# Gathered experts: u and v of an expert fetched as one 8 KB row instead of two 4 KB rows

## The chip, the cores and the metric

One core of a Trainium2 chip runs the kernel. The metric is device time in microseconds (us) of one execution; less is better. One execution was also taken by the hardware profiler, and all views below are of that one.

## What is computed

One layer of a diffusion backbone over 1024 latent tokens of width 1024: a token mixer (two recurrent scans), then PEER, a retrieval of experts. Only PEER is touched here. For each token, eight heads choose 16 experts each out of 16384, so 128 experts with an index and a gate. An expert is one row u and one row v of 1024 floats:

```
act = gelu(einsum('pd,ped->pe', hx, u_tab[ix]))        # one dot product per token and expert
y   = einsum('pe,ped->pd', gx * act, v_tab[ix])        # sum of 128 scaled rows v per token
x   = LN(ALPHA * x + g2 * y)
```

## The kernel before

The tokens form eight tiles of 128. PEER runs in two ways side by side.

**Dense tiles.** Tiles 0 to 4 (ND = 5, 640 tokens) are computed against all 16384 experts by TensorE, 128 steps of 128 experts. `dense_s` makes the products of h with u in a PSUM tile `S` (two halves of 24 matmuls) and ScalarE applies Gelu into `ge` (L1139). `dense_w` loads `vf`, splits it into two bf16 parts (ScalarE cast L1149, then a subtraction on POOL, L1150, that reads two SBUF tiles), multiplies `ge` by the gate matrix `G` (VectorE, L1152) and splits the product `w` (ScalarE L1154, VectorE L1155). `dense_y` sums four experts' w times v in a PSUM bank `y` (L1167), and VectorE adds it to `ya` in SBUF (L1174). `S` and `y` have three PSUM banks each. 66 of the 128 `S` steps are made ahead, while the gates are still being chosen, and spilled to DRAM.

**Gathered tiles.** Tiles 5 to 7 are computed by the class `Gather`, from rows fetched from DRAM by index: partition p receives the row that token p chose. `fetch` issues one indirect DMA on the POOL queue (L1075) for one of 256 steps of a tile: 128 rows u first, then 128 rows v, 4 KB for each partition, into a ring of six buffers `row` (ROWS). `use` takes the oldest. For a row u it is one VectorE instruction (L1094) that multiplies by h and sums into a column of `dot`; h lies in PSUM for this (copied once per tile, L1091). After 128 of them one Gelu on ScalarE (L1096) and one multiplication by the gates (L1097) serve the whole tile. For a row v it is one VectorE instruction (L1102) that adds the scaled row to a sum in the same two PSUM banks, `hg`. Their inputs in SBUF are thus one tile each, `row`; the other big operand is in PSUM.

`final` adds the residual, loads `xn` into a buffer of the same ring (L1110), normalizes and stores.

The order on each engine is set by a scheduler, from the program's order and its own estimate of times. `gather(n)` is called with a quota at each step of the other work: 100 rows while the scores are made (G0), 120 and 240 around the choice of gates (G1, G2), the rest of the 768 spread over the 128 dense steps. An engine works off its list in order: what waits at the head holds all behind it.

## Time and profile before

| what | value |
|---|---|
| median of 3 runs | 3173.94 us (3171.61 to 3189.06) |
| profiled execution, own time | 3190.5 us |
| its span, first to last instruction | 3188.7 us |
| busy: TensorE (PE), VectorE (DVE), POOL, ScalarE (ACT) | 91%, 79%, 58%, 37% |
| mean granted TensorE clock | 0.951 of 2.4 GHz |
| DMA: bytes, mean rate | 900.31 MB, 282 GB/s |

The gathered rows begin at about 1118 us, the matmuls of `dense_y` run from about 1900 to 3125 us, and the rest is the closing normalization. Busy shares are means over stages with different limits, so each stage is read by itself. PE busy counts the multiplying, with ends that are modelled; ACT, DVE, POOL busy count an instruction from its start to its end, with whatever held it up inside.

### The profile page before, as it was taken

The page shows a single profiled execution, that of the slowest core. Times are in us where ns is not written, and L with a number is a line of the kernel's source. Part 1 is how long each engine was busy: PE and PEld are TensorE (multiplying, and loading weights), DVE is VectorE, ACT ScalarE, POOL GpSimd, SP SyncE. Part 2 cuts the span into 40 slices and gives each one's busy share as a digit, 9 for nine tenths or more (in the row PEclk, how much of TensorE's full clock was granted, in tenths as well). Part 3 has the DMA queues.
Part 4 walks back from the last instruction along what each step waited for, and adds up shares of the span by engine and source line. Part 5 has one row for each costly group of instructions (what it writes and reads, how often), then busy time and mean ns, then how long its engine had stood idle before and what let it go on. Part 6 is the DMA issues. An engine that isn't in the chain of part 4 may idle for free.

```text
span 3188.7 us, 50415 instructions
## 1 busy us (share of the span) xinstructions
PE 2914.0 (91%) x18799; PEld 1889.2 (59%) x18943; DVE 2534.5 (79%) x5328; ACT 1194.3 (37%) x1743; POOL 1838.4 (58%) x1358
## 2 busy tenths in 40 slices
PE   7898999997698899999999989999999999999992
PEld 3644556666586567677777865554555555545550
DVE  8434464798778899898877778888888888888898
ACT  4464463445345522136666642221222122212211
POOL 3565675422347466416665665766666666666664
PEclk8999997998899899999999999999999999999996
DMA  7688666421268699859888998999999999989985
GB/s 282 211 291 291 214 211 218 166 79 42 100 228 278 219 332 345 295 188 309 295 289 296 309 358 314 361 337 340 357 366 365 360 362 361 360 329 372 357 319 190
DMA packets 319546, 900.31 MB, mean 282 GB/s; under 512 B 28076, under 2 KB 107572, under 8 KB 311364
## 3 DMA queue, kind: packets, MB, share of 16 engines
q1 hardware_dynamic: 208708, 494.38, 44.5%
q0 software_dynamic: 110592, 402.70, 33.9%
q8 instruction: 149, 2.44, 0.3%
q14 instruction: 97, 0.79, 0.1%
HBM read 758.67 MB, written 138.30 MB: 281 GB/s over the span
## 4 chain that ended last, share of the span: by engine, by line
PE 23%; DVE 22%; DMA 10%; issue 8%; POOL 6%; ACT 2%; SPq 1%; DVEq 0%; POOLq 0%; ACTq 0%
PE y L1167 12%; PE S L1134 9%; DMA row<-in_peer_v_dram,idx 7%; DVE row L1094 4%; POOL row L1075 3%; DVE hg L1102 3%; DMA row<-in_peer_u_dram,idx 2%; PE y L1042 2%; DVE us L1037 2%; POOL vs L1150 1%; DVE alt L881 1%; DVE ind L883 1%; DMA us<-in_peer_ut_dram 1%; DVE w L1155 1%; DVE ind L880 1%
## 5 line engine op out<-in xcount | busy, mean ns | idle before, releaser
L1134 PE MATMUL S<-hTd,uT 128*128 128x320 f16 (+1 forms) x6144 | 886.0, 301 | 0.5 <-ACT ge L1139 0.5
L1167 PE MATMUL y<-vs,w 128*128 128x512 bf16 x3730 | 852.2, 381 | 26.9 <-DVE ya L1174 11.0
L1134 PEld LDWEIGHTS <-uT 128*128 128x128 bf16 x6144 | 604.1, 98 | 251.9 <-issue 1.6
L1167 PEld LDWEIGHTS <-w 128*128 128x128 bf16 x3840 | 377.3, 98 | 460.7 <-issue 32.2
L1102 DVE SCALAR_TENSOR_TENSOR hg<-row,dot,hg 128x1024 f32<-128x1024 f32 x381 | 489.7, 1285 | 120.8 <-DMA row<-in_peer_v_dram,idx 117.1
L1075 POOL DMA_INDIRECT row<-in_peer_u_dram,idx x384 | 388.8, 1012 | 294.2 <-DVE row L1094 151.6
L1094 DVE SCALAR_TENSOR_TENSOR row<-row,hg 128x1024 f32<-128x1024 f32 x384 | 459.7, 1212 | 65.7 <-DMA row<-in_peer_u_dram,idx 63.4
L1075 POOL DMA_INDIRECT row<-in_peer_v_dram,idx x384 | 383.6, 999 | 219.3 <-DVE hg L1102 149.5
L199 POOL TENSOR_TENSOR uT<-us,uT 128x1024 bf16<-128x1024 f32 x128 | 297.4, 2328 | 186.4 <-ACT uT L198 170.9
L1149 ACT CAST vs<-vf 128x1024 bf16<-128x1024 f32 x128 | 130.3, 1043 | 510.5 <-PE y L1167 292.6
L1150 POOL TENSOR_TENSOR vs<-vf,vs 128x1024 bf16<-128x1024 f32 x128 | 276.4, 2176 | 41.0 <-ACT vs L1149 29.6
L1038 POOL TENSOR_TENSOR kT<-us,gf 128x512 f32<-128x512 bf16 x160 | 177.9, 1133 | 193.7 <-DVE us L1037 171.3
L1139 ACT ACTIVATE ge<-S 128x320 f32<-128x320 f32 x256 | 112.7, 442 | 402.2 <-PE S L1134 401.0
L222 PE MATMUL pj<-xmT,wb 128*128 128x512 f16 (+3 forms) x1214 | 251.4, 358 | 3.1 <-DVE q L500 0.9
L230 PE MATMUL pj<-wb,xmT 128*128 128x256 f16 (+1 forms) x1728 | 217.4, 286 | 15.1 <-DVE rsg L751 5.2
L1174 DVE TENSOR_TENSOR ya<-ya,y 128x512 f32<-128x512 f32 x310 | 208.8, 681 | 26.9 <-PE y L1167 26.3
L230 PEld LDWEIGHTS <-xmT 128*128 128x128 f16 (+1 forms) x1968 | 184.9, 103 | 54.8 <-issue 16.5
L1043 ACT COPY gst<-y 128x512 f32<-128x512 f32 x160 | 171.1, 1075 | 88.0 <-PE y L1042 88.0
L222 PEld LDWEIGHTS <-wb 128*128 128x128 f16 (+1 forms) x1248 | 121.2, 99 | 125.6 <-issue 21.2
L198 ACT CAST uT<-us 128x1024 bf16<-128x1024 f32 x128 | 133.3, 1044 | 135.2 <-DMA us<-in_peer_ut_dram 103.8
L1037 DVE TENSOR_TENSOR us<-iob,eT 128x512 bf16<-128x512 bf16 x320 | 166.7, 569 | 18.2 <-ACT kT L1039 9.2
L1042 PE MATMUL y<-kT 128*128 128x128 f32 x1280 | 163.1, 279 | 11.2 <-ACT kT L1039 6.5
(389 smaller groups left out, 3866.9 us busy)
## 6 DMA issues: line engine op xcount, KB each, us to landing
us<-in_peer_ut_dram SPq DMA_DIRECT2D x128, 512.0 KB
Ud<-uT SPq DMA_DIRECT2D x128, 512.0 KB
uT<-Ud SPq DMA_DIRECT2D x128, 512.0 KB
vf<-in_peer_v_dram SPq DMA_DIRECT2D x128, 512.0 KB
Gd<-gst SPq DMA_DIRECT2D x20, 1984.0 KB
Gt<-Gd SPq DMA_DIRECT2D x31, 1280.0 KB
Sd<-ge SPq DMA_DIRECT2D x66, 320.0 KB
kT<-Sd SPq DMA_DIRECT2D x66, 320.0 KB
```

The lines of the kernel that those rows point to most:

```text
L199: nc.gpsimd.tensor_tensor(lo, uf, hi, op=OP.subtract)
L222: g.nc.tensor.matmul(ps[:, :t1 - t0], w.t[a][:, k, c0:c0 + 128], g.xmT[b][:, k, t0:t1], start=(k == 0 and a == b), stop=(k == KD - 1 and a ...
L230: g.nc.tensor.matmul(ps, g.xmT[a][:, k, t * 128:(t + 1) * 128], w.t[b][:, k, :w.n], start=(k == 0 and a == b), stop=(k == KD - 1 and a == 1))
L1037: nc.vector.tensor_tensor(cm[:, a], g.iob, eT[:, a, None, t0:t0 + 4].to_broadcast([128, 128, 4]), op=OP.is_equal)
L1042: nc.tensor.matmul(ps[:, i * 128:(i + 1) * 128], oh[:, 0, i], oh[:, 1, i], start=True, stop=True)
L1075: d = g.nc.gpsimd.indirect_dma_start(out=b, out_offset=None, in_=self.I["peer_u" if n < 128 else "peer_v"][0], in_offset=bass.IndirectOffs ...
L1094: nc.vector.scalar_tensor_tensor(b, b, 1.0, self.ps, op0=OP.mult, op1=OP.mult, accum_out=dot[:, j:j + 1])
L1102: nc.vector.scalar_tensor_tensor(self.ps, b, dot[:, j:j + 1], self.ps, op0=OP.mult, op1=OP.add)
L1134: m = nc.tensor.matmul(ps[:, :hn], uT[:, a, k, :], g.hTd[b][:, k, i * hn:(i + 1) * hn], start=(k == 0 and (a, b) == (0, 0)), stop=(k == KD ...
L1150: nc.gpsimd.tensor_tensor(v[:, 1], vf, v[:, 0], op=OP.subtract)
L1167: nc.tensor.matmul(ps, w[:, a, t * 128:(t + 1) * 128], v[:, b, h * 512:(h + 1) * 512], start=(n == 0), stop=(n == 3 * GI - 1))
L1174: nc.vector.tensor_add(ya, ya, ps)
```

## The change

The host lays out a new input, `peer_uv`: row e is u of expert e followed by v of expert e, 2048 floats. One indirect DMA now brings both (128 steps of a tile, 384 in all), into a ring of four buffers of 8 KB for each partition; the quotas G0, G1, G2 are halved. The dot product reads h from SBUF (`g.h`), and PSUM holds only the sum (`sums`, two banks, made with the first row v). Gelu and the gate are applied to one column at a time on ScalarE, two instructions of 128x1 for each row (L1096, L1097). The addition of a row v stands in the program one step behind its dot product (`behind`). To make room, `ge` has two buffers instead of four, and `vf` one of its own and one of the pool `up`.

```
-        b = g.grp.tile([128, D], F32, name="row")
-        d = g.nc.gpsimd.indirect_dma_start(out=b, out_offset=None, in_=self.I["peer_u" if n < 128 else "peer_v"][0],
-                                           in_offset=bass.IndirectOffsetOnAxis(ap=g.idx[:, t, n % 128:n % 128 + 1], axis=0))
+        b = g.grp.tile([128, 2, D], F32, name="row")
+        d = g.nc.gpsimd.indirect_dma_start(out=b.rearrange("p a d -> p (a d)"), out_offset=None, in_=self.I["peer_uv"],
+                                           in_offset=bass.IndirectOffsetOnAxis(ap=g.idx[:, t, n:n + 1], axis=0))
...
-            nc.vector.scalar_tensor_tensor(b, b, 1.0, self.ps, op0=OP.mult, op1=OP.mult, accum_out=dot[:, j:j + 1])
-            if j == 127:
-                nc.scalar.activation(dot, dot, AF.Gelu)
-                nc.vector.tensor_mul(dot, dot, g.gate[:, t, :])
+            self.h = g.h[:, t, :]
+        dot = self.dot[:, j:j + 1]
+        nc.vector.scalar_tensor_tensor(b[:, 0], b[:, 0], 1.0, self.h, op0=OP.mult, op1=OP.mult, accum_out=dot)
+        nc.scalar.activation(dot, dot, AF.Gelu)
+        nc.scalar.activation(dot, dot, AF.Copy, scale=g.gate[:, t, j:j + 1])
+        if self.behind:
+            self.add()
+        self.behind = (t, j, b[:, 1], dot)
+    def add(self):
+        if j == 0:
+            self.ps = g.pb.tile([128, 2, 512], F32, name="sums").rearrange("p a b -> p (a b)")
+            nc.vector.tensor_scalar(self.ps, v, dot, None, op0=OP.mult)
         else:
-                nc.vector.scalar_tensor_tensor(self.ps, b, dot[:, j:j + 1], self.ps, op0=OP.mult, op1=OP.add)
+            nc.vector.scalar_tensor_tensor(self.ps, v, dot, self.ps, op0=OP.mult, op1=OP.add)
...
-    xt = g.grp.tile([128, D], F32, name="row")
+    xt = g.grp.tile([128, 2, D], F32, name="row")[:, 0]
...
-ROWS = 6
+ROWS = 4
...
-G0 = 100
-G1 = 120
-G2 = 240
+G0 = 50
+G1 = 60
+G2 = 120
...
-        g.gep = pool("gep", 4)
+        g.gep = pool("gep", 2)
...
-        g.vfp = pool("vfp", 2)
+        g.vfp = pool("vfp", 1)
...
+        g.vf = [g.vfp.tile([128, D], F32, name="vf"), g.up.tile([128, 2, D], BF, name="us").rearrange("p a b -> p (a b)").bitcast(F32)]
...
+    ins["peer_uv"] = np.stack([ins["peer_u"][0], ins["peer_v"][0]], axis=1).reshape(-1, 2 * D)
```

Line numbers after the change: dot product L1095, Gelu L1096, gate L1097, addition L1110 (first row L1108), fetch L1078, load of xn L1118, residual L1121 (before L1113), Gelu of `S` L1147, cast and subtraction of v L1157 and L1158, `w` L1160 to L1163, `dense_y` L1175, `ya` L1182. TensorE's list keeps its pattern. Three places where the lists change:

VectorE in the middle of the dense steps, before (the numbers tell the buffers apart; `hg` is h in PSUM here):

```order
L1094 SCALAR_TENSOR_TENSOR row_22089,dot_19890<-row_22089,hg_19889 128x1024
L1094 SCALAR_TENSOR_TENSOR row_22092,dot_19890<-row_22092,hg_19889 128x1024
L1152 TENSOR_TENSOR ge_22459<-ge_22459,Gt_22455 128x640
L1094 SCALAR_TENSOR_TENSOR row_22095,dot_19890<-row_22095,hg_19889 128x1024
L1155 TENSOR_TENSOR w_22518<-ge_22459,w_22518 128x640
L1174 TENSOR_TENSOR ya_19456<-ya_19456,y_22521 128x512
L1094 SCALAR_TENSOR_TENSOR row_22098,dot_19890<-row_22098,hg_19889 128x1024
```

and after the change, in the same place (`h` is in SBUF, `sums` in PSUM):

```order
L1160 TENSOR_TENSOR ge_22744<-ge_22744,Gt_22740 128x640
L1110 SCALAR_TENSOR_TENSOR sums_19996<-row_22400,dot_19987,sums_19996 128x1024
L1095 SCALAR_TENSOR_TENSOR row_22499,dot_19987<-row_22499,h_7828 128x1024
L1163 TENSOR_TENSOR w_22802<-ge_22744,w_22802 128x640
L1182 TENSOR_TENSOR ya_19447<-ya_19447,y_22805 128x512
L1110 SCALAR_TENSOR_TENSOR sums_19996<-row_22499,dot_19987,sums_19996 128x1024
L1182 TENSOR_TENSOR ya_19447<-ya_19447,y_22819 128x512
L1095 SCALAR_TENSOR_TENSOR row_22505,dot_19987<-row_22505,h_7828 128x1024
L1110 SCALAR_TENSOR_TENSOR sums_19996<-row_22505,dot_19987,sums_19996 128x1024
L1160 TENSOR_TENSOR ge_22847<-ge_22847,Gt_22740 128x640
```

The addition of a row may stand right behind its own dot product (row_22505), although the program has it one step later. From the first `ya` instruction on there are 249 additions; 52 follow their dot product directly, 62 with one `ya` addition between.

ScalarE in the same stage, after the change (`ge<-S` is the Gelu of TensorE's product; before, the casts and these stood there alone):

```order
L1147 ACTIVATE ge_23078<-S_23079 128x320
L1096 ACTIVATE dot_19987<-dot_19987 128x1
L1097 ACTIVATE dot_19987<-dot_19987,gate_7834 128x1
L1147 ACTIVATE ge_23078<-S_23105 128x320
L1162 CAST w_23136<-ge_23078 128x640
L1096 ACTIVATE dot_19987<-dot_19987 128x1
L1097 ACTIVATE dot_19987<-dot_19987,gate_7834 128x1
L1157 CAST vs_23298<-vf_19442 128x1024
```

The two instructions of a dot product's column stand between instructions that wait for TensorE or for a load, and hold up those behind them until VectorE has the dot product.

VectorE at the end, after the change (row_29992 and row_30039 to row_30227 hold xn, loaded in the order 29992, 30039, 30086, 30133, 30180, 30227; row_29977 is the last gathered row):

```order
L1182 TENSOR_TENSOR ya_19447<-ya_19447,y_30213 128x512
L1095 SCALAR_TENSOR_TENSOR row_29977,dot_25046<-row_29977,h_7828 128x1024
L1120 TENSOR_TENSOR ya_19447<-ya_19447,hTg0_13693 128x512
L1110 SCALAR_TENSOR_TENSOR sums_25055<-row_29971,dot_25046,sums_25055 128x1024
L1120 TENSOR_TENSOR ya_19447<-ya_19447,hTg1_13696 128x512
L1121 SCALAR_TENSOR_TENSOR ya_19447<-row_30039,ya_19447 128x1024
L1110 SCALAR_TENSOR_TENSOR sums_25055<-row_29977,dot_25046,sums_25055 128x1024
L1121 SCALAR_TENSOR_TENSOR ya_19447<-row_30086,ya_19447 128x1024
L1120 TENSOR_TENSOR us_13699<-sums_25055,hTg0_13693 128x512
L1120 TENSOR_TENSOR us_13699<-sums_25055,hTg1_13696 128x512
L1121 SCALAR_TENSOR_TENSOR ya_19447<-row_30133,ya_19447 128x1024
L1121 SCALAR_TENSOR_TENSOR us_13699<-row_29992,us_13699 128x1024
```

Before, twelve additions of rows v stood behind the last `ya` addition; now one dot product and two additions do. With four buffers, row_30133 takes that of row_29977, and row_30180 that of row_29992, which the last instruction shown sets free.

## Rows read from the trace of the kernel before

**Rows 1.** Busy time of each engine in stretches (from:to, length; PE, weight load, DVE, ACT, POOL in us with instruction counts; granted clock, DMA busy share, GB/s).

```profile
1100.00:1300.00 200.00, 190.34 (x1472) 142.22 (x1471) 197.50 (x815) 57.31 (x111) 117.33 (x115) 0.98 0.86 315
...
1450.00:1900.00 450.00, 430.94 (x3439) 349.33 (x3437) 351.57 (x736) 285.39 (x431) 286.05 (x271) 0.99 0.93 310
...
1950.00:3080.00 1130.00, 1113.57 (x6011) 599.07 (x6111) 974.33 (x1282) 260.83 (x363) 749.68 (x600) 1.00 0.94 354
...
3125.00:3189.00 64.00, 0.15 (x1) 0.00 (x0) 50.75 (x59) 8.34 (x12) 28.70 (x16) 0.53 0.46 169
```

**Rows 2.** Two pieces of the chain that ended last, at the same place of two successive groups of four experts (start, length in us, what).

```profile
2902.34 10.09 PE y L1167 x46
...
2941.28 10.09 PE y L1167 x46
```

**Rows 3.** Groups of instructions from 1950 to 3080 us (line, engine, operation, tiles, shapes, count | busy us, mean ns of one | idle time before).

```profile
L1094 DVE SCALAR_TENSOR_TENSOR row<-row,hg 128x1024 f32<-128x1024 f32 x256 | 305.8, 1215 | 55.2 <-DMA row<-in_peer_u_dram,idx 53.0 <-ACT hg L1091 1.6
L1102 DVE SCALAR_TENSOR_TENSOR hg<-row,dot,hg 128x1024 f32<-128x1024 f32 x218 | 280.2, 1285 | 41.7 <-DMA row<-in_peer_v_dram,idx 39.3
L1150 POOL TENSOR_TENSOR vs<-vf,vs 128x1024 bf16<-128x1024 f32 x121 | 261.0, 2173 | 22.0 <-ACT vs L1149 20.6
...
L1174 DVE TENSOR_TENSOR ya<-ya,y 128x512 f32<-128x512 f32 x291 | 196.0, 681 | 26.9 <-PE y L1167 26.3
...
L1155 DVE TENSOR_TENSOR w<-kT,w 128x640 bf16<-128x640 f32 x64 | 70.0, 1137 | 0.0
L1152 DVE TENSOR_TENSOR kT<-kT,Gt 128x640 f32<-128x640 f32 x62 | 62.7, 1020 | 0.2 <-DMA Gt<-Gd 0.2
L1152 DVE TENSOR_TENSOR ge<-ge,Gt 128x640 f32<-128x640 f32 x54 | 48.3, 895 | 29.5 <-ACT ge L1139 29.2
L1155 DVE TENSOR_TENSOR w<-ge,w 128x640 bf16<-128x640 f32 x56 | 48.2, 861 | 0.0
```

**Rows 4.** What VectorE waited for from 1950 to 3080 us (total us, times, longest).

```profile
DVE row L1094 <- DMA row<-in_peer_u_dram,idx: 53.0, 46, 4.1
DVE hg L1102 <- DMA row<-in_peer_v_dram,idx: 39.3, 38, 2.5
DVE ge L1152 <- ACT ge L1139: 29.2, 28, 2.7
DVE ya L1174 <- PE y L1167: 26.3, 37, 1.9
```

**Rows 5.** What TensorE waited for from 1100 to 3189 us (total us, times, longest).

```profile
PE y L1167 <- DVE ya L1174: 11.0, 6, 3.6
...
PE y L1167 <- ACT vs L1149: 8.4, 1, 8.4
...
PE y L1042 <- POOL kT L1038: 4.2, 9, 1.5
```

**Rows 6.** Shortest, median and longest instruction of four lines, in ns, over the whole span.

```profile
L1155 DVE TENSOR_TENSOR w<-kT,w x66: 810/818/5214, 1924.5 to 3078.6; 128x640 bf16<-128x640 f32 x66
...
L1152 DVE TENSOR_TENSOR kT<-kT,Gt x66: 765/819/5228, 1917.8 to 3064.2; 128x640 f32<-128x640 f32 x66
...
L1094 DVE SCALAR_TENSOR_TENSOR row<-row,hg x384: 1168/1214/1223, 1122.3 to 2871.6; 128x1024 f32<-128x1024 f32 x192
...
L1150 POOL TENSOR_TENSOR vs<-vf,vs x128: 2121/2142/2770, 1901.9 to 3082.5; 128x1024 bf16<-128x1024 f32 x128
```

**Rows 7.** Instructions in order of time (start, length in us, engine, line): VectorE and POOL around 2258 us, then around 2796 us.

```profile
2256.43 4.23 POOL L1150 TENSOR_TENSOR vs<-vf,vs 128x1024 bf16<-128x1024 f32 x2
...
2258.08 1.22 DVE L1094 SCALAR_TENSOR_TENSOR row<-row,hg 128x1024 f32<-128x1024 f32 x1
...
2795.44 5.23 DVE L1152 TENSOR_TENSOR kT<-kT,Gt 128x640 f32<-128x640 f32 x1
2795.75 4.23 POOL L1150 TENSOR_TENSOR vs<-vf,vs 128x1024 bf16<-128x1024 f32 x2
```

**Rows 8.** The indirect DMAs: shortest, median and longest issue on POOL in ns, and the time from issue to landing over all 768.

```profile
L1075 POOL DMA_INDIRECT row<-in_peer_u_dram,idx x384: 935/941/2027, 1117.8 to 2856.9; - x192
...
DMA to landing us min/median/max: 4.1/7.7/14.5
```

**Rows 9.** A short ScalarE instruction of 128x1 and its successor on VectorE: shortest, median, longest in ns; then the two in order of time.

```profile
L149 ACT ACTIVATE lnrs<-lnmv,eps x8: 278/282/295, 1966.3 to 3166.1; 128x1 f32<-128x1 f32 x8
...
3165.88 0.47 ACT L149 ACTIVATE lnrs<-lnmv,eps 128x1 f32<-128x1 f32 x2
3166.19 0.35 DVE L150 RECIPROCAL lnrs<-lnrs 128x1 f32<-128x1 f32 x2 [2.31 <-ACT lnrs L149]
```

**Rows 10.** What ScalarE waited for from 1950 to 3080 us, one row (total us, times, longest).

```profile
ACT ge L1139 <- PE S L1134: 247.4, 103, 4.5
```

**Rows 11.** Groups of POOL instructions from 1100 to 1950 us that read two SBUF tiles (columns as in rows 3).

```profile
L1038 POOL TENSOR_TENSOR kT<-us,gf 128x512 f32<-128x512 bf16 x160 | 177.9, 1133 | 193.7 <-DVE us L1037 171.3 <-PE y L1042 17.9 <-PE S L1134 2.0
...
L77 POOL TENSOR_TENSOR uT<-us,uT 128x512 bf16<-128x512 f32 x28 | 32.0, 1163 | 29.8 <-ACT uT L76 20.8 <-PE y L982 8.8
```

**Rows 12.** The end in order of time: the last `ya` addition is at 3126.84, the last matmul ends at 3125.2; then the rows v, the loads of xn and the first residual.

```profile
3129.23 13.21 DVE L1102 SCALAR_TENSOR_TENSOR hg<-row,dot,hg 128x1024 f32<-128x1024 f32 x10
...
3137.17 9.71 SPq L1110 DMA_DIRECT2D row<-xn  x6
...
3145.30 1.23 DVE L1113 SCALAR_TENSOR_TENSOR ya<-row,ya 128x1024 f32<-128x1024 f32 x1 [2.86 <-DMA row<-xn]
```

More of the change, by code (lines that the diff above doesn't have):

```diff
@@ L1057, in __init__ @@
         self.n, self.m, self.rows = 0, 0, []
+        self.behind = None
         self.pinned = True
-        self.total = (NL - ND) * 256
+        self.total = (NL - ND) * 128
     def __call__(self, n):
@@ L1068, in __call__ @@
                 self.use()
+            if self.behind:
+                self.add()
     def fetch(self):
         g = self.g
[L1072 removed]
+        t, n = divmod(self.n, 128)
         self.n += 1
[L1074 to L1076 removed]
+        b = g.grp.tile([128, 2, D], F32, name="row")
+        d = g.nc.gpsimd.indirect_dma_start(out=b.rearrange("p a d -> p (a d)"), out_offset=None, in_=self.I["peer_uv"],
+                                           in_offset=bass.IndirectOffsetOnAxis(ap=g.idx[:, t, n:n + 1], axis=0))
         if self.pinned:
@@ L1082, in use @@
         g, nc = self.g, self.g.nc
[L1083 removed]
+        t, j = divmod(self.m, 128)
         self.m += 1
         b = self.rows.pop(0)
[L1086 to L1089 removed]
+        if j == 0:
+            if self.behind:
+                self.add()
+            self.h = g.h[:, t, :]
             self.dot = g.gyp.tile([128, 128], F32, name="dot")
[L1091 to L1104 removed]
+        dot = self.dot[:, j:j + 1]
+        nc.vector.scalar_tensor_tensor(b[:, 0], b[:, 0], 1.0, self.h, op0=OP.mult, op1=OP.mult, accum_out=dot)
+        nc.scalar.activation(dot, dot, AF.Gelu)
+        nc.scalar.activation(dot, dot, AF.Copy, scale=g.gate[:, t, j:j + 1])
+        if self.behind:
+            self.add()
+        self.behind = (t, j, b[:, 1], dot)
+    def add(self):
+        g, nc = self.g, self.g.nc
+        t, j, v, dot = self.behind
+        self.behind = None
+        if j == 0:
+            self.ps = g.pb.tile([128, 2, 512], F32, name="sums").rearrange("p a b -> p (a b)")
+            nc.vector.tensor_scalar(self.ps, v, dot, None, op0=OP.mult)
+        else:
+            nc.vector.scalar_tensor_tensor(self.ps, v, dot, self.ps, op0=OP.mult, op1=OP.add)
+        if j == 127:
+            final(g, self.out, ND + t, g.gy, self.ps)
 def final(g, out, t, y, src):
     nc = g.nc
[L1109 removed]
+    xt = g.grp.tile([128, 2, D], F32, name="row")[:, 0]
     nc.sync.dma_start(xt, g.xn[t])
@@ L1145, in dense_w @@
     nc = g.nc
-    vf = g.vfp.tile([128, D], F32, name="vf")
+    vf = g.vf[i2 % 2]
     nc.sync.dma_start(vf, I["peer_v"][0].rearrange("(a b) d -> a b d", b=128)[:, i2, :])
```

13 lines of the change are left out of this document (removed).

## The prediction

> **What bounds the kernel now.** I read the stretches first. From 1950 to 3080 us TensorE is busy 1113.6 of 1130 us at a granted clock of 1.00 [rows 1]; the chain that ended last runs there through TensorE alone, at one pace: the same piece starts at 2902.34 and at 2941.28 us, so a group of four experts takes 38.94 us [rows 2]. That stage is TensorE's, and the change takes no matmul away, so it can win next to nothing in it. What the reader should see is how little room VectorE has beside it: 974.3 of 1130 us busy, 156 us idle, of which 53.0 + 39.3 are waits for gathered rows and 29.2 + 26.3 waits that come from TensorE [rows 1, 4]. TensorE waits for VectorE only 11.0 us in all [rows 5]. VectorE keeps up with 14% to spare; the question is whether it still does. POOL is busy 750 of 1130 us there and waits mostly for buffers; it is not on the path, so halving its DMAs is worth little by itself. From 1100 to 1300 us VectorE is the full engine (197.5 of 200), from 1450 to 1900 TensorE again; after 3125 us only the closing arithmetic is left [rows 1].
>
> I work against the profiled execution (3190.5 us); the median of the runs, 3174, lies 16.5 us lower, and I move the difference over to it.
>
> **The dense stage, part by part.** Rows are counted in the stretch 1950 to 3080: 256 u and 218 v [rows 3], so 237 pairs.
>
> *Fetch.* 384 issues fewer on POOL, some 0.94 us each [rows 8]. Whether an issue of 8 KB rows costs 0.94 us (as many rows) or 1.9 (as many bytes) is not shown; both are no more than now and POOL waits for buffers anyway, so I take 0 for either. What arrives late is another matter (below).
>
> *Plain VectorE work.* One dot product and one addition per pair, as before: 1.22 and 1.29 us. h from SBUF in place of PSUM costs nothing by itself: the residual instruction, of the same operation and width with both inputs in SBUF, takes 1.23 us [rows 12] beside 1.215 [rows 3].
>
> *VectorE against POOL.* This is the term on which the forecast rests. The splitting of v on POOL takes 261.0 us of the 1130, 23% [rows 3], in pairs of 4.23 us [rows 7]. A dot product with h in PSUM runs through such a pair in 1.22 us, and never takes over 1.223 [rows 6, 7]. A VectorE instruction with two inputs in SBUF doesn't: the one at 2795.44 takes 5.23 us, until the pair on POOL is over, where its median is 0.82 [rows 6, 7]. The four groups of that sort cost 229.2 us for 236 instructions where 0.82 each would be 193.5: 35.7 us lost already, 0.15 us each [rows 3, 6]. The change makes 237 dot products to instructions of this sort. Lower end: 0.15 each, 36 us. Upper end: VectorE stands through every splitting, 261 less the 36 already paid, 225 us. Between: a start falls into a splitting with chance 0.23 and then waits for the end of one (half of 2.17, 1.1 us) or of the pair (2.1 us), mean 1.6, so 0.37 us each, **88 us**. I take that, since VectorE has an instruction of this sort every few us after the change.
>
> The rows show this for TENSOR_TENSOR alone. The Trainium skill (SBUF — State Buffer, "SBUF: two separate sides") has it for any VectorE operation with two SBUF inputs against a GpSimd operation that reads SBUF: an exclusive lock, held for the whole instruction. By that rule the dot product is caught too, and the term is the 88 us; by the rows of TENSOR_TENSOR alone, read narrowly, it could be 0, and the stage would stay at 1130 us. This trace agrees as far as it goes (5.23 us against 0.82).
>
> *VectorE waits for ScalarE.* Between a dot product and its addition there are now two instructions of 128x1. Such a one takes 0.28 us, and its successor on VectorE begins some 0.07 us after it [rows 9]: 2 x 0.28 + 2 x 0.07 = 0.7 us. Of 249 additions 52 stand right behind their dot product; 62 have a `ya` addition of 0.68 us between [rows 3], which covers it. So 52 x 0.7 = **36 us**; with 1.0 us for the trip, 71. Beyond that ScalarE can be at a cast, or hold at the head of its list for TensorE, as it did 247.4 us before [rows 10]. Lower end 0, upper end 247.4/1130 of the 237 pairs at half a mean wait of 2.4 us, 62 us; I take **15**, since the list has the column where its time should come.
>
> *Waits for rows.* A ring of six 4 KB rows at one row per 38.94/16.5 = 2.4 us becomes four of 8 KB at one per 4.7 us. A buffer's round is issue 1, landing, dot product 1.2, trip 0.7, addition 1.3. Landing was 7.7 us for half as many bytes [rows 8]; between 7.7 and 15.4, I take 11. The round is then 15 us, over four 3.8 us, against 4.7 needed: enough, with less room than before (10 us over six, 1.7 against 2.4). Waits were 92 us; a VectorE that is later finds more rows there. Ends 0 and 92, I take half, **46**.
>
> Sum for VectorE: 974 + 88 + 36 + 15 + 46 = 1159 us against 1130, **+29 us**. Its waits for TensorE (55 us) are gone in this sum: it is VectorE that is late, `y` banks come free late, and TensorE waits for the `ya` addition. With all lower ends it is 1046, less than the stage, and the change costs nothing.
>
> **Before and after that stage.** From 1100 to 1300 us some 50 dot products fall; splittings on POOL take 32.0 us of the 200 there, 1.16 us each [rows 11], so 50 x 0.16 x 0.58 = 5 us, and direct successors some 5 us more: 10 at the full engine, 0 if TensorE's own products (190 of 200 busy) are the limit; I take **+8**. From 1450 to 1900 POOL's products take 177.9 of 450 us in pieces of 1.13 [rows 11]; 70 dot products x 0.40 x 0.57 = 16 us, which the 98 us that VectorE has free cover: **+1**. The smaller `ge` and `vf` rings I cost at nothing: `ge` is needed again a group later, `vf` still has two buffers.
>
> The end: twelve additions of rows v behind the last `ya` addition, ten of them 13.21 us [rows 12], so 15.6 us, become one dot product and two additions, 3.8: -12. But six loads of xn went out together at 3137 and cost VectorE one wait of 2.86 us; with four buffers two of the six go later, one behind the gathered tile's own residual. A landing takes 4.1 us at least [rows 8]; two or three such waits less the arithmetic between are 7 to 14 us, so +4 to +11, I take +6. Together **-6**.
>
> 29 + 9 - 6 = +32: 3190.5 becomes 3222.5, and the median **3206 us**, 1.0% slower.
>
> **The rivals.**
> A (my forecast): VectorE fills up. With the lock at 150 us, the trip at 71, the queue at 30 and 20 for rows it is 1245, +115; so A reaches from +17 to +116.
> B: it is absorbed. The lock costs near its lower end (or doesn't catch this operation) and the waits for rows shrink by as much as is added. For it: 156 us idle and only 11.0 us of TensorE waiting. Against it: 5.23 us where 0.82 is normal. It decides where lock, trip, queue and rows stay under 156 us. Time 3158 to 3190, by its middle 3174.
> C: the ring. With a landing of 18 us the round is 22 us, 5.6 us per pair against 4.7: 237 x 0.9 = +213 us, 3387; and a late row now holds ScalarE as well, whose Gelu of `S` frees TensorE's banks. For it: the longest landing, 14.5 us for 4 KB rows. Against it: the median. The Trainium skill (DMA: Bandwidth & Descriptors, "Measured") has 6.15 us for 1 MB, one such fetch; by that the ring never binds, but 7.7 us for half of it here speaks against relying on it.
> D, the other side: faster. POOL is relieved of half its issues, so what TensorE waits for behind POOL, `vs` and `ya` (11.0 + 8.4 + 4.2 = 24 us [rows 5]) goes, and the end gives its 12 us without the loads' 6: -30 to -36, about 3141. It needs the lock and the trip to fit into VectorE's idle time with room left, so that `ya` comes earlier than now: under about 60 us in sum. For it: fewer, longer transfers. Against it: in the dense stage TensorE has but 16 us to give back.
>
> **Chances and range.** A 0.52, B 0.28, C 0.08, D 0.12. A measurement here can tell about 0.5% (16 us) from no change: faster 0.12 (D), same 0.28 (B), slower 0.60 (A, C). The range takes in A and B, 3160 to 3290, and leaves C and D out; A alone is 3190 to 3290.
>
> **What would show it.** Right: dot products of 2 to 5 us in the new profile while POOL splits v, and a mean well over 1.22; VectorE over 93% busy from 1950 on; TensorE waiting for `ya` by several times 11.0 us and a period over 38.94; VectorE waiting for the gate instruction of 128x1 some 30 to 70 us in all; at the end one or two waits for xn behind the gathered residual. Wrong: dot products that stay at 1.22 us beside POOL (then B), a period of 38.94 with VectorE still idle by 10% (B or D), or waits for rows that grow past 200 us with landings over 15 us (C).

## The result, and the profile after

| | before | after |
|---|---|---|
| median of the runs shown | 3173.94 us | 3220.99 us (3213.31 to 3221.54) |
| profiled execution, span | 3190.5, 3188.7 us | 3213.3, 3211.5 us |
| ratio to before | | 1.0118, 95% interval 1.0088 to 1.0148 |
| the same kernel once more, five rounds | 3188.74 us | 3223.05 us, ratio 1.0096 (1.0066 to 1.0125) |

One of the six runs of the changed kernel in the last row took 5033.59 us at a granted clock of 0.554; that row's median counts it, the ratio does not. By the ratios the kernel is 1.0 to 1.2% slower (the quotient of the two medians of three runs, 1.0148, lies at the upper end of the interval); the forecast was 3206 us, 1.0%. The sign and the size came as forecast, but most of the loss lies in a stage that the forecast costed at +1 us. I cut the span at TensorE's own marks: the first and the last matmul of the gate stage (L1042) and of `dense_y`. The rows give count, shortest/median/longest in ns, and the first and last start in us; first of before:

```profile
L1042 PE MATMUL y<-kT x1280: 272/275/442, 1422.7 to 1877.9; 128*128 128x128 f32 x183
L1167 PE MATMUL y<-vs,w x3730: 376/379/634, 1901.9 to 3124.8; 128*128 128x512 bf16 x197
```

and of after:

```profile
L1042 PE MATMUL y<-kT x1280: 272/275/553, 1423.2 to 1907.7; 128*128 128x128 f32 x183
L1175 PE MATMUL y<-vs,w x3726: 376/379/634, 1934.8 to 3160.2; 128*128 128x512 bf16 x197
```

Differences of these starts, and of the span, give the stages of every kernel below ("again" is the second profile of after):

| us | to the first L1042 | gate stage | to `dense_y` | `dense_y` | tail |
|---|---|---|---|---|---|
| before | 1422.7 | 455.2 | 24.0 | 1222.9 | 63.9 |
| after | 1423.2 | **484.5** | 27.1 | 1225.4 | **51.3** |
| after, again | 1428.5 | **488.4** | 26.8 | 1231.1 | 51.7 |

The gate stage lost 29 to 33 us, the dense stage 2.5 to 8, and the tail gave back 12. The stretches after, to be held against [rows 1] (last line: the tail):

```profile
1100.00:1300.00 200.00, 184.05 (x1421) 137.04 (x1419) 195.42 (x720) 70.27 (x188) 83.08 (x69) 0.97 0.84 310
...
1450.00:1900.00 450.00, 419.11 (x3304) 337.44 (x3302) 333.23 (x761) 290.13 (x525) 243.03 (x207) 0.99 0.87 289
...
1950.00:3080.00 1130.00, 1108.86 (x5995) 597.70 (x6100) 1044.59 (x1255) 359.78 (x831) 600.89 (x359) 1.00 0.93 354
```

```profile
3160.00:3211.50 51.50, 0.54 (x3) 0.05 (x1) 40.83 (x53) 10.62 (x17) 21.39 (x8) 0.53 0.34 127
```

In the dense stage VectorE went from 974 to 1045 us busy, as forecast, and TensorE stayed at 1109 of 1130 (1114 before); in the chain the same piece starts 77.88 us apart over two groups, still 38.94 us for each [rows 2]:

```profile
2353.42 10.09 PE y L1175 x46
...
2431.30 10.09 PE y L1175 x46
```

**The lock is there.** Groups from 1950 to 3080 us (columns as in [rows 3]), then shortest, median and longest dot product, then VectorE and POOL around 2637 us:

```profile
L1095 DVE SCALAR_TENSOR_TENSOR row<-row,h 128x1024 f32<-128x1024 f32 x236 | 344.0, 1458 | 1.7 <-DMA row<-in_peer_uv_dram,idx 1.6
L1110 DVE SCALAR_TENSOR_TENSOR sums<-row,dot,sums 128x1024 f32<-128x1024 f32 x233 | 298.9, 1283 | 44.7 <-ACT dot L1097 44.4
```

```profile
L1095 DVE SCALAR_TENSOR_TENSOR row<-row,h x384: 1195/1217/5627, 1119.2 to 3163.5; 128x1024 f32<-128x1024 f32 x192
```

```profile
2637.01 5.63 DVE L1095 SCALAR_TENSOR_TENSOR row<-row,h 128x1024 f32<-128x1024 f32 x1
2637.33 2.13 POOL L1158 TENSOR_TENSOR vs<-vf,vs 128x1024 bf16<-128x1024 f32 x1
2639.41 2.13 POOL L1158 TENSOR_TENSOR vs<-us,vs 128x1024 bf16<-128x1024 f32 x1
```

A dot product that never took over 1.223 us [rows 6] here stands through a pair of splittings on POOL, 5.63 us, the longest case. The median is hardly changed; the mean is 1.458 us, so 236 x 0.243 = 57 us. Counted in the same trace, 42 of the 236 took over 1.3 us, 30 over 2 us and one over 4 us. VectorE's waits in the same stretch, against [rows 4]:

```profile
DVE sums L1110 <- ACT dot L1097: 44.4, 62, 3.2
DVE ya L1182 <- PE y L1175: 26.0, 41, 1.2
DVE ge L1160 <- ACT ge L1147: 10.3, 8, 1.8
DVE row L1095 <- DMA row<-in_peer_uv_dram,idx: 1.6, 1, 1.6
```

The waits for rows, 92 us before, are all but gone; the round trip over ScalarE took their place. The landing of a row of 8 KB was 8.6 us in the median, beside 7.7 for 4 KB [rows 8], and the issue hardly longer:

```profile
L1078 POOL DMA_INDIRECT row<-in_peer_uv_dram,idx x384: 935/1050/2148, 1113.1 to 3155.0; - x192
...
DMA to landing us min/median/max: 5.4/8.6/14.5
```

**The gate stage.** What TensorE, ScalarE and VectorE waited for; TensorE from 1100 us to the end [rows 5], the others from 1420 to 1910 us (us in total, times, longest):

```profile
PE y L1042 <- ACT kT L1039: 33.0, 42, 3.1
PE y L1175 <- DVE ya L1182: 15.9, 6, 4.8
```

```profile
ACT dot L1096 <- DVE row L1095: 102.1, 56, 6.7
```

```profile
DVE row L1095 <- DMA row<-in_peer_uv_dram,idx: 64.9, 27, 4.7
DVE us L1037 <- ACT kT L1039: 39.2, 51, 2.6
```

TensorE waits for the cast `kT` (L1039) on ScalarE, 33.0 us where it was 6.5 before. ScalarE stands 102.1 us, with a column at the head of its list, waiting for a dot product that is not done. Counted wait by wait in the same trace, in 26 of the 56 (55.5 us) VectorE had itself just waited for the row; in the other 30 (46.7 us) it had not. VectorE was idle for a row in only 22.5 us of the 102.1; in some 65 us it was at work on dot products. One case with a late row, in order of time (start, length, engine, line; idle before it):

```profile
1664.95 1.23 DVE L1095 SCALAR_TENSOR_TENSOR row<-row,h 128x1024 f32<-128x1024 f32 x1 [4.35 <-DMA row<-in_peer_uv_dram,idx]
...
1666.22 0.20 ACT L1096 ACTIVATE dot<-dot 128x1 f32<-128x1 f32 x1 [3.02 <-DVE row L1095]
1666.33 1.01 ACT L1043 COPY gst<-y 128x512 f32<-128x512 f32 x1
...
1667.14 0.64 ACT L1039 CAST kT<-us 128x512 f32<-128x512 bf16 x1
...
1667.93 1.13 PE L1042 MATMUL y<-kT 128*128 128x128 f32 x8 [1.51 <-ACT kT L1039]
```

Read from the top: VectorE waits 4.35 us for its row; ScalarE, idle, waits 3.02 us with the column of 128x1 at the head; the copy of `gst` and the cast behind it come late, and TensorE stands 1.51 us.

POOL's products there (L1038, columns as in [rows 11]) became longer as well, 1242 ns in the mean where they were 1133:

```profile
L1038 POOL TENSOR_TENSOR kT<-us,gf 128x512 f32<-128x512 bf16 x160 | 195.3, 1242 | 266.7 <-DVE us L1037 163.3 <-PE y L1042 93.8 <-DVE bs L879 3.4
```

**The tail.** Before, ten additions [rows 12]; after, the last dot product and two additions between the residuals, and one wait of 0.44 us for xn:

```profile
3163.48 1.22 DVE L1095 SCALAR_TENSOR_TENSOR row<-row,h 128x1024 f32<-128x1024 f32 x1
...
3168.16 1.28 DVE L1110 SCALAR_TENSOR_TENSOR sums<-row,dot,sums 128x1024 f32<-128x1024 f32 x1
3169.88 1.22 DVE L1121 SCALAR_TENSOR_TENSOR ya<-row,ya 128x1024 f32<-128x1024 f32 x1 [0.44 <-DMA row<-xn]
```

### The profile page after: what moved, and what is told of

Its sections match the earlier page's. It is cut to its first block, busy times and chain, and to the rows that moved or that the text cites. A ratio compares the mean times of both kernels' runs of the same rounds, so it can differ in the third digit from the quotient of the medians.

```text
span 3211.5 us, 50255 instructions
## 1 busy us (share of the span) xinstructions
PE 2916.5 (91%) x18795; PEld 1887.7 (59%) x18943; DVE 2613.8 (81%) x5325; ACT 1348.6 (42%) x2505; POOL 1596.8 (50%) x974
## 4 chain that ended last, share of the span: by engine, by line
PE 30%; DVE 23%; DMA 9%; issue 5%; ACT 3%; POOL 2%; DVEq 0%; SPq 0%; ACTq 0%; another core or an unknown queue 0%; POOLq 0%
PE y L1175 20%; PE S L1142 9%; DMA row<-in_peer_uv_dram,idx 7%; DVE row L1095 4%; DVE sums L1110 4%; DVE us L1037 2%; DVE alt L881 1%; POOL kT L1038 1%; DMA us<-in_peer_ut_dram 1%; DVE w L1163 1%; DVE ind L883 1%; ACT gst L1043 1%; DMA Gd<-gst 1%; DVE ind L880 1%; DVE ya L1182 1%
## 5 line engine op out<-in xcount | busy, mean ns | idle before, releaser
L1175 PE MATMUL y<-vs,w 128*128 128x512 bf16 x3726 | 854.2, 382 | 31.8 <-DVE ya L1182 15.9
L1078 POOL DMA_INDIRECT row<-in_peer_uv_dram,idx x384 | 490.7, 1278 | 628.9 <-DVE sums L1110 455.3
L1175 PEld LDWEIGHTS <-w 128*128 128x128 bf16 x3840 | 377.8, 98 | 463.7 <-issue 39.4
L1095 DVE SCALAR_TENSOR_TENSOR row<-row,h 128x1024 f32<-128x1024 f32 x384 | 536.7, 1398 | 73.1 <-DMA row<-in_peer_uv_dram,idx 72.9
L1110 DVE SCALAR_TENSOR_TENSOR sums<-row,dot,sums 128x1024 f32<-128x1024 f32 x381 | 488.2, 1281 | 68.1 <-ACT dot L1097 66.5
L1096 ACT ACTIVATE dot<-dot 128x1 f32<-128x1 f32 x384 | 77.7, 202 | 818.5 <-DVE row L1095 817.5
L1038 POOL TENSOR_TENSOR kT<-us,gf 128x512 f32<-128x512 bf16 x160 | 195.3, 1242 | 266.7 <-DVE us L1037 163.3
L1182 DVE TENSOR_TENSOR ya<-ya,y 128x512 f32<-128x512 f32 x310 | 208.3, 679 | 28.9 <-PE y L1175 27.7
L1037 DVE TENSOR_TENSOR us<-iob,eT 128x512 bf16<-128x512 bf16 x320 | 169.1, 571 | 42.7 <-ACT kT L1039 39.2
L1042 PE MATMUL y<-kT 128*128 128x128 f32 x1280 | 170.5, 283 | 34.5 <-ACT kT L1039 33.0
L1158 POOL TENSOR_TENSOR vs<-vf,vs 128x1024 bf16<-128x1024 f32 x64 | 149.4, 2334 | 92.0 <-ACT vs L1157 91.5
L1042 PEld LDWEIGHTS y<-kT 128*128 128x128 f32 x1280 | 157.5, 195 | 48.1 <-issue 40.9
L1147 ACT ACTIVATE ge<-S 128x320 f32<-128x320 f32 x256 | 111.1, 436 | 132.3 <-PE S L1142 126.8
```

Source lines behind the costliest of these rows:

```text
L1037: nc.vector.tensor_tensor(cm[:, a], g.iob, eT[:, a, None, t0:t0 + 4].to_broadcast([128, 128, 4]), op=OP.is_equal)
L1038: nc.gpsimd.tensor_tensor(oh[:, 0].rearrange("p t e -> p e t"), cm[:, 0], gf[:, None, t0:t0 + 4].to_broadcast([128, 128, 4]), op=OP.mult)
L1042: nc.tensor.matmul(ps[:, i * 128:(i + 1) * 128], oh[:, 0, i], oh[:, 1, i], start=True, stop=True)
L1078: d = g.nc.gpsimd.indirect_dma_start(out=b.rearrange("p a d -> p (a d)"), out_offset=None, in_=self.I["peer_uv"], in_offset=bass.IndirectO ...
L1095: nc.vector.scalar_tensor_tensor(b[:, 0], b[:, 0], 1.0, self.h, op0=OP.mult, op1=OP.mult, accum_out=dot)
L1110: nc.vector.scalar_tensor_tensor(self.ps, v, dot, self.ps, op0=OP.mult, op1=OP.add)
```

## Experiments

Theory 1: ScalarE's list hands a late dot product on to TensorE. Theory 2: the lock. All ratios are to the kernel before on the same chip, with 95% intervals; stage times are of one profiled execution each.

Each edit was scheduled anew, and the traces show what that did to the order on VectorE and ScalarE. In 3 and 8 it came out as in the kernel without the edit, so these are repeats; in 4 it is that of the kernel before in all but a few places; in 5 it is that of 2 from the gate stage on. In 2, 6, 7 and 9 to 12 it changed together with the edit. What the new order alone is worth was not tested there.

**1. The changed kernel again** (no edit).

> The changed kernel once more, as the yardstick for the other kernels of this group on the same chip. Expected: 1.009 to 1.015 of the kernel before, with TensorE's first dense_y matmul (L1175) some 30 us later than before and the dense period at 38.94 us.

Measured: 3223.05 us, 1.0096 (1.0066 to 1.0125); first `dense_y` 42 us later than in the profile of before, of which 6 us lie ahead of the gate stage.

**2. No columns.**

```
-        nc.scalar.activation(dot, dot, AF.Gelu)
-        nc.scalar.activation(dot, dot, AF.Copy, scale=g.gate[:, t, j:j + 1])
```

> The changed kernel without the two ScalarE instructions of 128x1 per row (Gelu and gate of the gathered tiles are left out, the raw dot product scales the row v); fetch, dot product from SBUF, additions and all else stay. Theory 1 (ScalarE's list: the columns stand at its head, wait for a late row and hold up the kT cast and the gst copy that TensorE needs in the gate stage): TensorE's waits for kT L1039 fall from 33.0 us to under 10, the first dense_y matmul comes 20 to 30 us earlier, and the time is 3175 to 3195 us, 0.8 to 1.2% under the changed kernel. Theory 2 (the lock between the dot product and POOL's products): the dot products still read two SBUF tiles, so the gate stage stays as it is, within 5 us, and the time stays 1.0 to 1.4% over the kernel before. Both expect the dense period to stay at 38.94 us; VectorE's waits for the dot column (44.4 us) are gone.

Measured: 3201.51 us, 1.0033 (1.0015 to 1.0051). The gate stage is back at 457.6 us, and TensorE's wait for `kT` at 10.2 us; the dense stage stays at 1231.9 us:

```profile
L1042 PE MATMUL y<-kT x1280: 272/275/553, 1428.8 to 1886.4; 128*128 128x128 f32 x183
L1173 PE MATMUL y<-vs,w x3840: 376/379/634, 1916.7 to 3148.6; 128*128 128x512 bf16 x192
```

What follows: the columns are a cause in the gate stage, though POOL's products there take longer still (1274 ns in the mean, 1133 before). Whether by ScalarE's waiting or by its work, this edit does not tell, since it takes both away. The whole came out 6 us over the range expected, because of the dense stage.

**3. Rows fetched further ahead.**

```
-AHEAD = 2
+AHEAD = 3
...
-        if self.behind:
-            self.add()
         self.behind = (t, j, b[:, 1], dot)
+        self.add()
```

> The changed kernel with a row used when three are fetched behind it instead of two, and its addition in the program right behind its own dot product; four buffers as before, all arithmetic kept. Theory 1 (late rows hold ScalarE's list): a row has landed more often when its column comes to the head of the list, so ScalarE's waits for the dot product from 1420 us to the first dense_y (102.1 us in the changed kernel) fall by half or more, and the gate stage gets back 10 to 25 us; time 3190 to 3210. Theory 2 (lock): no difference in the gate stage beyond 5 us, time within 0.3% of the changed kernel. A third way: a ring of four with three ahead leaves no free buffer, each fetch then waits for an addition, and rows come later than now: slower by 10 us or more.

Measured: 3226.03 us, 1.0107 (1.0081 to 1.0134). ScalarE still waits 100.5 us for the dot product, VectorE 64.0 us for rows. The lists came out as in the changed kernel, so no row was fetched earlier: it says nothing on the theories and is a third profile of the changed kernel (gate stage 489.1, `dense_y` 1229.7 us). A longer ring wasn't tried.

**4. The kernel before with h in SBUF.**

```
...
-            nc.scalar.copy(self.ps, g.h[:, t, :])
...
-            nc.vector.scalar_tensor_tensor(b, b, 1.0, self.ps, op0=OP.mult, op1=OP.mult, accum_out=dot[:, j:j + 1])
+            nc.vector.scalar_tensor_tensor(b, b, 1.0, g.h[:, t, :], op0=OP.mult, op1=OP.mult, accum_out=dot[:, j:j + 1])
```

> The kernel before with one edit: the dot product reads h from SBUF and not from its PSUM copy; rows of 4 KB, one Gelu and one gate per tile, six buffers stay. This is the lock alone. Theory 1: the dot products grow from 1.215 to about 1.45 us in the mean beside POOL's splitting, with single ones over 4 us, but the gate stage loses under 8 us and the time is within 0.4% of the kernel before. Theory 2 (lock as the cause): the gate stage is 20 to 30 us longer and the time 0.8 to 1.2% over the kernel before.

Measured: 3265.28 us, 1.0243 (1.0212 to 1.0273): neither. The loss is in the dense stage, 1274.7 us (+52 to the profile of before, +47 to that of the eighth experiment), and its gate stage, 457.8 us, says nothing of the lock, since from 1420 to 1910 us this kernel makes 116 additions and only eight dot products. The stage, then dot products and what TensorE waited for, from 1950 and from 2110 to 3080 us:

```profile
L1165 PE MATMUL y<-vs,w x3840: 376/379/634, 1916.3 to 3191.0; 128*128 128x512 bf16 x192
```

```profile
L1092 DVE SCALAR_TENSOR_TENSOR row<-row,h 128x1024 f32<-128x1024 f32 x256 | 392.4, 1555 | 41.8 <-DMA row<-in_peer_u_dram,idx 41.4
```

```profile
PE y L1165 <- DVE ya L1172: 48.6, 25, 3.7
```

and two stretches of the same profile, the first of dot products alone, the second of additions alone (columns as in [rows 1]):

```profile
2653.00:2801.00 148.00, 135.19 (x748) 72.84 (x746) 135.53 (x179) 28.59 (x42) 109.60 (x73) 1.00 0.89 317
2948.00:3104.00 156.00, 156.00 (x867) 84.64 (x866) 133.75 (x142) 33.94 (x49) 104.39 (x86) 1.00 0.97 364
```

With dot products TensorE is busy 135 of 148 us and VectorE 92%; with additions TensorE is busy throughout. The lock's 0.34 us for each of 256 is 87 us, not much over the 57 us of the changed kernel, but here it falls on some half of the stage, with two dot products where the changed kernel has one and one addition. Since the order is almost that of the kernel before, this is the cleanest measurement of the lock.

**5. Columns that wait for nothing.**

```
+        c = g.fp.tile([128, 1], F32, name="col")
-        nc.scalar.activation(dot, dot, AF.Gelu)
+        nc.scalar.activation(c, g.gate[:, t, j:j + 1], AF.Gelu)
-        nc.scalar.activation(dot, dot, AF.Copy, scale=g.gate[:, t, j:j + 1])
+        nc.scalar.activation(c, c, AF.Copy, scale=g.gate[:, t, j:j + 1])
```

> The changed kernel with the same two ScalarE instructions of 128x1 per row at the same place of the program, but reading the gate and writing a scratch column, so that they wait for no dot product and no addition waits for them (the raw dot product scales the row v, as in the second kernel). This separates ScalarE's wait from ScalarE's work. If the wait at the head of ScalarE's list is the cause: as the kernel without columns, TensorE's waits for kT L1039 under 12 us (35 in the changed kernel), first dense_y matmul near 1917 us, time 3195 to 3205. If the work itself (2 x 0.25 us for each of some 70 rows in the gate stage, 35 us on ScalarE) is the cause: waits for kT of 25 us or more, first dense_y near 1940, time 3215 to 3230.

Measured: 3203.13 us, 1.0039 (1.0022 to 1.0057), gate stage 459.6 us, wait for `kT` 11.3 us: as without columns. But the columns do not stand where they should. Since they wait for nothing, the scheduler put all 384 ahead of the gate stage, between 1103 and 1287 us:

```profile
L1097 ACT ACTIVATE col<-gate x384: 186/198/226, 1103.2 to 1286.5; 128x1 f32<-128x1 f32 x192
```

From the gate stage on, VectorE's and ScalarE's lists are those of the second experiment. So this is a second measurement of that kernel, and it does not separate waiting from work. The trace of the changed kernel speaks for the waiting, as an attribution and not as an experiment. I took the 42 casts `kT` that TensorE waited for, each from the moment when its input was there and its buffer free (the end of the comparison L1037 and of the matmuls that read the buffer before) to its start. In that time ScalarE stood idle for a dot product for 61.8 us and worked on columns for 12.2 us.

**6. The column a step later.**

```
...
+        if self.behind:
+            self.column()
         nc.vector.scalar_tensor_tensor(b[:, 0], b[:, 0], 1.0, self.h, op0=OP.mult, op1=OP.mult, accum_out=dot)
-        nc.scalar.activation(dot, dot, AF.Gelu)
-        nc.scalar.activation(dot, dot, AF.Copy, scale=g.gate[:, t, j:j + 1])
...
+    def column(self):
+        g = self.g
+        t, j, v, dot = self.behind
+        c = g.nc.scalar.activation(dot, dot, AF.Gelu)
+        if self.pinned:
+            g.tc.keep_in_program_order(c)
+        g.nc.scalar.activation(dot, dot, AF.Copy, scale=g.gate[:, t, j:j + 1])
```

> The changed kernel, all arithmetic kept, with the column's Gelu and gate one step of the gather later in the program (ahead of the next row's dot product), and before the dense stage pinned behind the ScalarE instructions that the program has in between. If the wait at the head of ScalarE's list is the cause: ScalarE's wait for the dot product in the gate stage falls from 100 us to under 40, TensorE's waits for kT to under 18, the first dense_y matmul comes 10 to 25 us earlier and the time is 3200 to 3215. If it is the work: no change beyond 5 us. Against it: a row's buffer is held longer, so later fetches; if that decides, VectorE's waits for rows grow past 90 us and the time rises.

Measured: 3229.18 us, 1.0126 (1.0107 to 1.0145). ScalarE's wait fell only to 79.6 us, the wait for `kT` to 28.9 and the gate stage to 479.7, and TensorE now waited 12.6 + 9.0 us for the Gelu of `S`, where 4.1 us stood in the first experiment: for the most part moved, not removed.

**7. The lock taken away.**

```
-        nc.vector.scalar_tensor_tensor(b[:, 0], b[:, 0], 1.0, self.h, op0=OP.mult, op1=OP.mult, accum_out=dot)
+        nc.vector.scalar_tensor_tensor(b[:, 0], b[:, 0], 1.0, self.ps if j > 1 else self.h, op0=OP.mult, op1=OP.mult, accum_out=dot)
```

> The changed kernel with the dot product's second operand in PSUM: from the third row of a tile on it reads the bank of the sums in place of h (the sums then mean nothing); two ScalarE instructions per row, 8 KB rows and ring stay. This takes the lock alone away. Dot products go back to 1.215 us in the mean (1.46 in the changed kernel). If the lock is absorbed where dot products and additions alternate: dense period 38.94 us as it is, gate stage still 25 to 35 us longer than before, time within 0.3% of the changed kernel. If the lock is what costs: the time falls by 20 us or more, to that of the kernel before.

Measured: 3192.01 us, 1.0004 (0.9989 to 1.0019). The second branch: by the ratios the time drops by some 29 us (0.9%), with the columns still there.

```profile
L1042 PE MATMUL y<-kT x1280: 272/275/422, 1429.2 to 1898.3; 128*128 128x128 f32 x183
L1175 PE MATMUL y<-vs,w x3730: 376/379/634, 1920.9 to 3135.5; 128*128 128x512 bf16 x197
```

```profile
L1095 DVE SCALAR_TENSOR_TENSOR row<-row,sums 128x1024 f32<-128x1024 f32 x235 | 285.8, 1216 | 67.2 <-DMA row<-in_peer_uv_dram,idx 66.8
```

```profile
L1038 POOL TENSOR_TENSOR kT<-us,gf 128x512 f32<-128x512 bf16 x160 | 177.9, 1135 | 281.1 <-DVE us L1037 200.0 <-PE y L1042 78.1 <-DVE bs L882 1.4
```

The gate stage is 469.1 us (15 to 20 less than in the three profiles of the changed kernel), `dense_y` 1214.6 (11 to 16 less), VectorE's waits for rows are back at 66.8 us, and POOL's products at 1135 ns. So the lock is a cause in both stages, as far as the new order is not. That order shows at the end: behind the last `ya` now stand four dot products and five additions, where the changed kernel has one and two, and the tail is 59.4 us instead of 51.

**8. The kernel before, quotas a little earlier.**

```
-            gather(G2 + (n + 1) * (gather.total - G2) // 128)
+            gather(min(G2 + (n + 1) * (gather.total - G2) // 124, gather.total))
```

> The kernel before, all arithmetic kept, with the last 528 rows spread over 124 of the 128 dense steps, so that the last gathered row comes some 30 to 40 us earlier than the last dense_y. This is the tail alone: in the changed kernel the time behind the last dense_y matmul fell from 63.9 to 51 us. Expected: the twelve additions (15.6 us) leave the path, VectorE's rate of rows rises by 3%, which its idle time covers; 3162 to 3182, 0.2 to 0.5% under the kernel before. If VectorE's additional rate binds, or the tail is set by the loads of xn instead: no change.

Measured: 3194.23 us, 1.0004 (0.9988 to 1.002). The edit didn't do what it says: ten additions still stand in one piece (3148.19, 13.21 us) behind the last `ya`, and the lists are those of the kernel before. It tells nothing of the tail, but its gate stage, 455.3, and its `dense_y`, 1228.0 us, are second values for the form of before (its profile is of the slowest of its twelve runs, 3209.26 us).

**9. Neither lock nor columns** (edits 2 and 7 together).

> The changed kernel without the lock (dot product against the bank of the sums in place of h from the third row of a tile on) and without the two ScalarE instructions per row (Gelu and gate left out): what is left of the change is the 8 KB fetch, the ring, the mix of dot products and additions and the shorter tail. Each cause alone gave back 31 us (lock) and 21 us (column) of the 31 us lost. If the two multiply (the lock makes the dot product late, and the column hands its lateness to ScalarE), the pair gives little over the lock alone: the gate stage falls from 469 us (lock off) to 455 to 460, time 3176 to 3190 and 0 to 0.4% under the kernel before. If they add: 31 + 21 us, time 3165 to 3175, 0.5 to 0.8% under the kernel before.

Measured: 3182.51 us, 0.9988 (0.9974 to 1.0003); gate stage 453.4, `dense_y` 1212.9, tail 58.6 us. The profile is of the fastest of its twelve runs (3173.20 us).

```profile
L1042 PE MATMUL y<-kT x1280: 272/275/423, 1420.3 to 1873.7; 128*128 128x128 f32 x183
L1173 PE MATMUL y<-vs,w x3840: 376/379/634, 1899.6 to 3112.5; 128*128 128x512 bf16 x192
```

The four kernels together:

| | ratio | gate stage | `dense_y` | wait for `kT` |
|---|---|---|---|---|
| neither (9) | 0.9988 | 453.4 | 1212.9 | 7.4 |
| lock alone (2) | 1.0033 | 457.6 | 1231.9 | 10.2 |
| columns alone (7) | 1.0004 | 469.1 | 1214.6 | 23.6 |
| both (after, again) | 1.0096 | 488.4 | 1231.1 | 35.1 |

In the gate stage each alone costs 4 and 16 us, both 35 (31 by the first profile of after): more than the sum, the first branch of what was expected. In `dense_y` the lock costs 16 to 19 us (11 by that first profile), the columns 2 or nothing. These are single profiles, of kernels whose lists differ in more than the edit.

**10. h in PSUM, S and y with two banks each.**

```
...
-            self.h = g.h[:, t, :]
+            self.h = g.pb.tile([128, 2, 512], F32, name="hg").rearrange("p a b -> p (a b)")
+            nc.scalar.copy(self.h, g.h[:, t, :])
...
-        ps = g.pb.tile([128, 512], F32, name="S", bufs=3)
+        ps = g.pb.tile([128, 512], F32, name="S", bufs=2)
...
-    ps = g.pb.tile([128, 512], F32, name="y", bufs=3)
+    ps = g.pb.tile([128, 512], F32, name="y", bufs=2)
```

> The changed kernel with h of the gathered tile back in PSUM (two banks, one copy per tile on ScalarE) beside the sums, paid for with the banks of S and y: two each instead of three. All arithmetic kept. Dot products at 1.215 us again. If the third banks matter little: 3185 to 3200 us, level with the kernel before. If TensorE needs them: its waits for ya (dense) and for gst copies (gate stage) grow past 60 us together and the time is over 3230.

Measured: 3242.56 us, 1.0182 (1.0163 to 1.0202). Dot products are at 1.213 us, but TensorE waits 35.2 us for `ya`, and `dense_y` takes 1258.9 us. The two banks for h give the dot products their pace back, but the two taken from `S` and `y` cost more than that.

**11. h as 16-bit floats in one PSUM bank**, S with two banks, y with three.

```
...
-            self.h = g.h[:, t, :]
+            tmp = g.grp.tile([128, 2, D], F32, name="row").rearrange("p a d -> p (a d)").bitcast(F16)
+            hh = tmp[:, 0:D]
+            nc.scalar.copy(hh, g.h[:, t, :])
+            for r in range(2):
+                self.h = g.pb.tile([128, D], F16, name="hg")
+                for k in range(KD):
+                    nc.tensor.transpose(self.h[:, k * 128:(k + 1) * 128], hh[:, k * 128:(k + 1) * 128], g.ident16)
+                if r == 0:
+                    hh = tmp[:, D:2 * D]
+                    nc.scalar.copy(hh, self.h)
...
```

> The changed kernel with h of the gathered tile in one PSUM bank as 16-bit floats (rounded; brought there by two rounds of eight transposes on TensorE per tile, with one slot of the row ring as scratch), y keeps three banks, S has two. Dot products at 1.215 us if a 16-bit operand runs at the same pace and the lock is gone with it. If S's third bank is idle: 3182 to 3198 us, within 0.3% of the kernel before and 0.8 to 1.2% under the changed kernel. If S needs it: TensorE's waits for the Gelu of S (4 us in the changed kernel) grow past 30 us and the time stays over 3210.

Measured: 3192.01 us, 1.0022 (1.0007 to 1.0037), with all the arithmetic done (h rounded). This is the lock removed in a whole kernel, in an order that is neither that of the changed kernel nor that of the seventh: gate stage 471.7, `dense_y` 1213.5 us, as there, and dot products never over 1.246 us:

```profile
L1104 DVE SCALAR_TENSOR_TENSOR row<-row,hg x384: 1192/1215/1246, 1129.1 to 3142.3; 128x1024 f32<-128x1024 f32 x192
```

**12. Edits 11 and 6 together.**

> The kernel with h as 16-bit floats in PSUM (the eleventh), with the column of a row one gather step later in the program, pinned behind ScalarE's own work before the dense stage, as in the sixth kernel; all arithmetic kept. With the lock gone, dot products are in time more often, so a column that stands a step later should find them done: ScalarE's wait for the dot product in the gate stage falls from 83 us to under 50, the gate stage from 472 us to 458 to 466, and the time is 3176 to 3190, level with the kernel before or up to 0.3% under it. If the row's landing and not the lock sets the column's lateness: ScalarE's wait stays over 70 us and the time is 3190 to 3205.

Measured: 3200.29 us, 1.0065 (1.004 to 1.009). ScalarE's wait stays at 69.7 us, the gate stage at 474.5: the second branch, at its edge. In 41 of the 69.7 us VectorE was at work on dot products and in 17 idle for a row, so this does not show that the row's landing sets the wait. No version here beats the kernel before by more than a measurement can tell.

## Why the prediction came out

Right in sign and size (3206, measured 3221), and in one mechanism: two SBUF inputs beside POOL's work. The path from there to the time was wrong. The step that failed is the one that laid the loss in time: the dense stage at +29, where 2.5 to 8 us were measured, and "From 1450 to 1900" at +1, where 29 to 33 were. That these two add up to the right total is luck. By the prediction's own signs its rival A, a VectorE that fills up and holds TensorE, did not come: VectorE was busy 92.4% and not over 93, TensorE waited for `ya` 15.9 us and not several times 11.0, and the period stayed at 38.94. What came of the signs are the dot products over 2 us and the wait for the column.

- **Lock, +88 us for VectorE.** There, and smaller: 57 us on the dot products (0.24 us each for 0.37), some 66 us on all of VectorE (1044.6 against 978.3 us in the same stretch of the seventh experiment). Of 236 dot products 42 were held up, 0.18 for 0.23, by 1.4 us in the mean for 1.6. Starts that are not as random as I took them could be the reason; no run tested that. By the Trainium skill's rule (SBUF — State Buffer, "SBUF: two separate sides") the operation is caught too; the trace agrees (5.63 us against 1.22).
- **Trip and queue, 36 + 15 us.** 44.4 us measured, 62 waits of 0.72 us. (Rows 9 give 0.03 us behind a short instruction, not 0.07; and 22 us over four buffers are 5.5, not 5.6, and rival A's upper end is +118, not +116. None of these moves the forecast.)
- **Rows' waits, 46 us.** 1.6 measured: the mis-sized term. A VectorE that is later finds every row there; I wrote so and then took half. With 1.6 the forecast sum, 974 + 88 + 51 + 2, is 1115, under 1130, and my rival B's condition is met (57 + 44 + 2 us under 156). Beside before, the dense stage lost 2.5 to 8 us for 29 forecast.
- That is no proof that the lock was free there. Three kernels without it run `dense_y` in 1213 to 1215 us, where two profiles of the form of before have 1222.9 and 1228.0. So the rest of the change seems to gain some 8 to 15 us there, and the lock took them: half of rival D was true. What the gain consists of, the new order of the lists included, was not separated.
- **Gate stage, +1 us.** 29 to 33 measured, the greater part of the loss. I counted VectorE's 98 free us as cover. Two things were not costed. The column puts an unfinished dot product at the head of ScalarE's list, and the cast and the copy that TensorE needs stand behind it; the section on the change and rival C named that holding up, but the sum priced ScalarE's list for the dense stage alone. Without the lock this costs 16 us; the lock without it costs 4; together they cost 31 to 35. Part of that shows in ScalarE's wait for the dot product (97 to 102 us with both, 83 to 87 in experiments 7 and 11). The lock also has another side: POOL's products (L1038) became longer, 1133 to 1242 ns in the mean, 160 x 0.109 = 17 us; but TensorE's waits for them were only 0.6 us in the changed kernel (4.2 before, 7.2 without columns), so what that adds is not shown. Before, rows were late there too (77.8 us of VectorE's waits from 1420 to 1910 us), but only VectorE stood.
- **Landing, 11 us; ring.** 8.6 us measured, so rival C is out. The Trainium skill's 6.15 us for 1 MB (DMA: Bandwidth & Descriptors, "Measured"), which is the DMA engines' busy time alone, lies near the shortest landing, 5.4 us, and under the median: the measurement decides.
- **1100 to 1300, +8 us.** Up to the gate stage 0.5 and 5.8 us in the two profiles.
- **End, -6 us.** -12: the additions left as counted, but the loads of xn, forecast at +6, cost 0.44 us at the first residuals.

Open: what makes a row late in the gate stage (ring, POOL's list or the DMA itself), and how much of ScalarE's wait would go with it, since no edit brought the rows earlier; ScalarE's waiting against its work, which only the attribution above tells apart; and what each edit's new order is worth by itself.

## What to carry to other kernels

Before giving a small step to an in-order engine, ask what stands behind it there and for whom: its cost here was less its 0.2 to 0.3 us than the lateness that it passed on, and free time on the engine that is late gave no cover for that. When an operand moves from PSUM to SBUF, count the POOL work that reads SBUF beside it, on both engines, and place it: spread over all groups it cost 11 to 19 us of the dense stage, packed into some half of them 47 to 52. And cost a change in every stage through which the changed work runs, with the wait that ends last in that stage. When an edit is to test a cause, look in the new trace whether the order came out as meant: two of these edits changed nothing, and one took its instructions out of the stage.
